# Order of the value products, a mask product with all its rows, and weights in smaller pieces, in a two-layer transformer block on one core

## The chip, the cores and the metric

The kernel runs on one core of a Trainium2 chip, as one program. TensorE multiplies matrices, VectorE, ScalarE and GpSimd do elementwise work, SyncE (SP) issues DMAs, and so does ScalarE's own queue. The metric is the device time of one execution in microseconds; the less the better.

## What is computed

Two layers over 512 latent tokens of width 1024 and 256 context tokens. Each layer normalises and modulates the tokens, projects them (`w_in`, 2976 columns) and splits the columns over four mixers of four heads of 64: latent attention (keys and values come from a narrow latent vector), retention forwards and backwards, neighbourhood attention on an 8 x 64 grid, and sliding-window attention with sink logits. Their outputs are joined and projected (`w_out`); a gated FFN of 2816 hidden units follows. The parts that the change touches:

```python
def softmax_attend(q, k, v, scale, sink=None):
    s = jnp.einsum('bhqd,bhkd->bhqk', q, k, preferred_element_type=jnp.float32) * scale
    ...
    p = jax.nn.softmax(s, axis=-1)
    ...
    return jnp.einsum('bhqk,bhkd->bhqd', p.astype(v.dtype), v)

def na_mixer(xq, xk, xv, yq, yk, yv, rpb):
    ...
    col_in = (c[None, :] >= c0[:, None]) & (c[None, :] < c0[:, None] + NA_KC)
    ...
    s_loc = jnp.where(col_in[:, None, :], s_loc, NEG_INF)
    ...

def reference(x, c, ctx, c_ctx, ada_w, ...):
    for l in range(DEPTH):
        ...
        mx, my = token_mixers(hx @ w_in[l], hy @ w_in[l], row, col, ...)
        x = x + gx1 * (mx @ w_out[l])
        hx = rms_norm(x, norm2_g[l]) * (1.0 + scx2) + shx2
        x = x + gx2 * swiglu(hx, ffn_w1[l], ffn_w3[l], ffn_w2[l])
        ...
    return rms_norm(x, final_norm_g)
```

## The kernel before, in words

Tokens come in six tiles of 128 (0 to 3 the grid, 4 and 5 the context); the last layer only finishes the four of the grid. All data is float32. Large products are made of three (`mm3`, L455 to L457): both operands are split into a rounded high part and a low remainder, and high times high, high times low and low times high are summed in PSUM. A weight comes into a `raw` buffer by DMA; `split_unit` then lets ScalarE make the high part `wh` (L435) and VectorE, each third time GpSimd, the low part `wl` (`sub_lo`, L201). `raw` has 2 buffers of 2048 elements a partition (1 MB), `wh` 5 and `wl` 7 of 1024.

The order in which a layer is written down: `na_proj` (the blocks of `w_in` for the neighbourhood's keys and values and for its queries), `na_attn`, `swa_proj`, `swa_attn`, `ret_proj`, `mla_proj` with the latent attention tile by tile, the output projection in parts between them (`rest`, `finish`), and the FFN in 11 groups of 256 hidden units (`tr_units` loads W1 and W3, then W2 follows). `load_nat` loads a block of `w_in` or `w_out` in two DMAs of up to four blocks of 128 rows each, from SP's queue; `tr_units` and the W2 load take ScalarE's. An engine executes its instructions in a fixed order, which a scheduler draws up when the program is built: it takes what is ready by its own reckoning, earlier written work first. So products of the next projection stand between the steps of an attention. A DMA that waits for a free buffer holds up what stands behind it on its queue.

Attention works on one tile of 128 queries and one head at a time: scores into PSUM, their minimum, the exponential on ScalarE (the scores carry a minus sign), the division by the sums (`norm_p`, L601), and `attend_T`, which transposes the probabilities block by block on TensorE (L567): ScalarE copies the first four blocks out of PSUM (L570), VectorE what comes after them (L572). When both heads of a pair have their transposed blocks `PTs`, `attend_pv` (L580) multiplies them with the values, the even head into the lower half of the output's partitions, the odd one into the upper half, so that each product has 64 stationary columns. There are 2, 4, 5 or 6 blocks of keys: 2 for context queries, 4 in the neighbourhood attention, 4 or 5 in the window, 6 in the latent attention.

In `na_attn` the columns outside the neighbourhood get a large number added to their score by a product (L918) of a 16-row indicator `naone` with a 16-row `namask`, behind the two products of queries and keys (L916, L917) and before those with the context's keys (L614). `swa_attn` does the like with the identity and `swmask`, of 128 rows (L1126, L1128), behind L1123 and L1124. Both masks are filled in `late_consts`.

Of the kernel before, what the change touches and what calls it, by code (L numbers as in the profile page):

```python
# [75 lines left out]

def build(tc, I, out, opts=None):
    nc = tc.nc
# [124 lines left out]
    # ---------------- constants  # L203
# [5 lines left out]
    naone = C("naone", [16, P], BF16)  # L209
    namask = C("namask", [16, 3, 32], BF16)  # L210
# [8 lines left out]
    def vec_tile(i, srcs):  # L219
        """rows of 128 values of the named vectors -> columns"""  # L220
        a = T("nat", [P, P])
        r = 0
        for name, src in srcs:
            n = src.shape[0] // P
            VROW[name] = (i, r)
            sp.dma_start(a[r:r + n, :], src.rearrange("(k p) -> k p", p=P))
            r += n
        ps = PS("u")
        pe.transpose(ps[:, 0:r], a[0:r, :], ident[0:r, 0:r])
        dve.tensor_copy(vecs[i], ps[:, 0:r])  # L230
# [5 lines left out]
    def late_consts():  # L236
        vec_tile(1, [("b1", I["ada_b"][1]), ("g1_1", I["norm1_g"][1]), ("g2_1", I["norm2_g"][1]),
                     ("qn0", I["mla_q_norm"][0]), ("kn0", I["mla_kv_norm"][0]),
                     ("qn1", I["mla_q_norm"][1]), ("kn1", I["mla_kv_norm"][1])])
        sp.dma_start(rope64, I["k_rope64"])  # L240
        sp.dma_start(rope32, I["k_rope32"])
        a = T("nat", [P, 96])
        sp.dma_start(a[0:16, :], I["k_namask"])
        act.activation(namask, a[0:16, :].rearrange("p (a b) -> p a b", a=3), AF.Copy)
        a = T("nat", [P, 2, P])
        sp.dma_start(a, I["k_swmask"])
        act.activation(swmask, a, AF.Copy)
        a = T("nat", [P, P])
        sp.dma_start(a[0:16, :], I["k_naone"])
        act.activation(naone, a[0:16, :], AF.Copy)  # L250
        act.activation(identb, ident, AF.Copy)
        s = I["swa_sink"]
        sp.dma_start(sink, bass.AP(tensor=s.tensor, offset=s.offset, ap=[[0, P], [H, LAYERS], [1, H]]))
        pool.tensor_scalar(sinkn, sink, -1.0, 1.0, op0=ALU.mult, op1=ALU.mult)

    # ---------------- small helpers
    def rsqrt(a, n, nm):
        """a [P, n] holds mean square; returns 1/sqrt(a)"""
        y = S("rs_y" + nm, n)
        u = S("rs_t" + nm, n)  # L260
        dve.tensor_scalar(y.bitcast(I32), a.bitcast(I32), 1, None, op0=ALU.logical_shift_right)
        dve.tensor_scalar(y.bitcast(I32), y.bitcast(I32), -1, 0x5F3759DF, op0=ALU.mult, op1=ALU.add)
        for _ in range(3):
            dve.tensor_tensor(u, y, y, op=ALU.mult)
            dve.scalar_tensor_tensor(u, u, -0.5, a, op0=ALU.mult, op1=ALU.mult)
            dve.scalar_tensor_tensor(y, u, 1.5, y, op0=ALU.add, op1=ALU.mult)
        return y

    def rsqrt1(a, nm):
        """a [P, 1]: 1/sqrt(a), times RS1"""  # L270
        y = S("rs_y" + nm, 1)
        u = S("rs_t" + nm, 1)
        dve.tensor_scalar(y.bitcast(I32), a.bitcast(I32), 1, None, op0=ALU.logical_shift_right)
        dve.tensor_scalar(y.bitcast(I32), y.bitcast(I32), -1, 0x5F3759DF, op0=ALU.mult, op1=ALU.add)
        for c in (-3.0, -12.0, -768.0):
            dve.scalar_tensor_tensor(u, y, a, y, op0=ALU.mult, op1=ALU.mult)
            dve.scalar_tensor_tensor(y, u, c, y, op0=ALU.add, op1=ALU.mult)
        return y

    # ---------------- adaLN modulation  # L280
# [5 lines left out]
    def mod_finish(l, v, s, k0, n):  # L286
        """bias, and for a scale (1 + scale) * g, of n feature blocks from k0"""
        m = modT[l][:, s, SLOT[v], k0:k0 + n]
        b = vec("b%d" % l, VT.index(v) * 8 + k0, n)
        dve.tensor_tensor(m, m, b, op=ALU.add)  # L290
        if v[1] == "c":
            dve.scalar_tensor_tensor(m, m, 1.0, vec("g%s_%d" % (v[2], l), k0, n), op0=ALU.add, op1=ALU.mult)
# [11 lines left out]
    def ada_first(q, ws):  # L304
        """shift and scale of the first norm of layer 0, features 256 * q and on"""
# [24 lines left out]
    def ada_rest(l, vs, wtag, depth, tag="u"):  # L330
        """vectors of layer l; a generator, a load and the products of an earlier load in each step"""
# [25 lines left out]
    def ada_sums(l, vs, wtag, depth, tag="u", atag="PT", after=None):  # L357
        """as ada_rest; the products are summed over the blocks of features before the tensor engine adds up partitions"""
# [72 lines left out]
    # ---------------- weights  # L431
# [7 lines left out]
    def load_nat(w, c0, n, ks=range(8)):  # L439
        """w [1024, *] DRAM -> list over k of (hi, lo) APs [128, n]"""  # L440
        res = []
        v = w.rearrange("(k p) n -> p k n", p=P)
        for kh in range(ks[0], ks[-1] + 1, 4):
            kn = min(4, ks[-1] + 1 - kh)
            raw = T("raw", [P, kn, n])
            Q["wn"].dma_start(raw, v[:, kh:kh + kn, c0:c0 + n])
            for u in range(0, kn, 2):
                hi, lo = split_unit(raw[:, u:u + 2, :], [2, n])
                for i in range(2):
                    res.append((hi[:, i, :], lo[:, i, :]))  # L450
        return res

    def mm3(ps, a, b, first, last):
        """ps += (a_hi + a_lo) (b_hi + b_lo)"""
# [4 lines left out]
    # ---------------- normalised, modulated, transposed activations  # L459
    def norm_stats(t, inplace=False):  # L460
        """normalised token tile t, as 8 blocks of 128 features"""
# [47 lines left out]
    def nat_block(w, c0, n, hT, order, rng=None, filler=None, nf=0, nxt=None):  # L509
        """generator over (t, psum) of natural outputs; rng(t) -> (a, b) columns wanted;  # L510
        nxt: first column and width of the block whose weights are loaded ahead"""
# [14 lines left out]
    def first_block(hT, order, parts):  # L526
        """as nat_block, all tiles together, the contraction in four parts"""
# [21 lines left out]
    def rope(out, ps, g, hd, t, tab):  # L549
        """out, ps: [P, g*hd] (out SBUF)"""  # L550
# [8 lines left out]
    # ---------------- softmax attention for one query tile and head  # L559
    def attend_T(Pm, nblk):  # L560
        """Pm [P, nblk*128] unnormalised -> its transposed blocks"""
# [13 lines left out]
    def attend_pv(pv, hp, PTs, vs):  # L575
        """heads 2 hp and 2 hp + 1 side by side: pv[:, 128 hp:128 hp + 128] = values^T of both"""
        n = len(vs[0])
        for i in range(n):
            for e in range(2):
                pe.matmul(pv[64 * e:64 * e + 64, hp * P:hp * P + P], vs[e][i], PTs[e][:, i, :],  # L580
                          start=(i == 0), stop=(i == n - 1), tile_position=(0, 64 * e))

    def norm_p(Pm, sums):
        """divide the rows by their sums, which come in parts [P, n]"""
# [18 lines left out]
    def put(pv, dst):  # L603
        """transposed outputs of 4 heads, two by two on the partitions, to dst [P, 2, 128]"""
# [5 lines left out]
    def scores(ps, q, k):  # L610
        """ps = q^T k from operands that are split and stacked: q, k lists of (stationary, moving)"""
# [4 lines left out]
    def soft_y(q_of, k_of, v_of, negsink=None, sk=None):  # L616
        """context queries of one tile: 4 heads on 256 keys"""
# [25 lines left out]
    def q_stack(src, scale):  # L643
        """src: 256 columns in DRAM -> stationaries [q_hi; q_hi], [q_lo; q_lo] of 4 heads, times scale"""
# [13 lines left out]
    def k_split(src, n, r=None):  # L658
        """src [P, n*64] natural, times r [P, 1] -> [P, n, 2, 64], hi and lo of each head"""
# [10 lines left out]
    def k_stack(dst, kd, n, t, tag="u"):  # L670
        """kd [P, n, 2, 64] natural, hi and lo -> dst[i][:, tile t] = [k_hi; k_lo]"""
# [6 lines left out]
    # ================= layers  # L678
# [31 lines left out]
    # startup  # L710
# [53 lines left out]
    # retention decays: log_sigmoid of both layers; [P, l, 8] and head-half layout [P, l, pair, dir]  # L764
# [27 lines left out]
    for l in range(LAYERS):  # L792
# [10 lines left out]
        # DRAM scratch of this layer  # L803
        o_d = DT(f"o_d{l}", [NT, 256])          # ret
        oT_d = DT(f"oT_d{l}", [512, NT])        # na | swa, transposed
        q_d = DT(f"q_d{l}", [NT, 640])          # mla: nope 256, rope 128 | swa 256
        qn_d = DT(f"qn_d{l}", [NT, 256])        # na, the grid in tiles of 16 columns
        r_d = DT(f"r_d{l}", [NT, 1280])         # ret q | k | v | gates f | gates b
        v_d = DT(f"v_d{l}", [NX, 256])          # na v of the grid
# [11 lines left out]
        def na_proj():  # L821
# [76 lines left out]
            def na_attn():  # L898
# [5 lines left out]
                for cb in range(4):  # L904
# [6 lines left out]
                    for h in range(H):  # L911
# [6 lines left out]
                        pe.matmul(loc, naone, namask[:, et:et + 1, :].to_broadcast([16, 8, 32]), start=False, stop=True)  # L918
# [23 lines left out]
        def mla_proj(R):  # L942
# [60 lines left out]
            def k_rope(t):  # L1003
                """the shared rope keys of the grid (t = 3) or of the context (t = 5)"""
# [277 lines left out]
        def m_pair(p, b):  # L1282
            """the operand of token tiles 2 p and 2 p + 1: b = 0 for mla | ret, 1 for na | swa"""
# [31 lines left out]
        # ---------- mixers  # L1315
# [22 lines left out]
        # ---------- output projection  # L1338
# [71 lines left out]
        # ---------- FFN  # L1410
# [17 lines left out]
        for g in range(11):  # L1428
            c0 = g * 256

            def tr_units(v):
                raw = T("raw", [P, 8, 256])
                Q["wf"].dma_start(raw, v[:, :, c0:c0 + 256])
                us = [split_unit(raw[:, 4 * u:4 * u + 4, :], [4, 256]) for u in range(2)]
# [31 lines left out]
            raw = T("raw", [P, 2, D])  # L1466
            Q["wf"].dma_start(raw, I["ffn_w2"][l, c0:c0 + 256, :].rearrange("(k p) n -> p k n", p=P))
            for j in range(2):
                down.append((gh[j], gl[j], split_unit(raw[:, j], [D])))
# [42 lines left out]
```

## Time and profile before

| what | value |
|---|---|
| median of 3 runs | 1955.18 us (1953.36 to 1959.28) |
| profiled execution, first to last instruction | 1949.8 us |
| median of the runs less that span | 5.4 us |
| TensorE busy | 1862.3 us, 96% |
| VectorE busy | 1205.8 us, 62% |
| ScalarE busy | 691.4 us, 35% |
| GpSimd busy | 614.8 us, 32% |
| moved by DMA | 215.46 MB, mean 111 GB/s |

The profiled execution's own time is known as its span from the first to the last instruction; what lies around it is taken as the distance to the runs' median. A busy time counts an engine's instructions and not its waits. The ends of matmuls are modelled and overlap, so their cost is better read from one start to the next. A float32 product of L580 stands in the trace as two matmuls. `po`, `pg`, `ps`, `pt`, `pu` are PSUM tiles, `PEld` is TensorE's load of the stationary operand, and `x22` says that 22 like instructions in a row were merged.

### The profile page before, as it was taken

To read this page: it belongs to the slowest core of one execution; us is meant where nothing else is said; L and a number is where in the kernel's file an instruction comes from. 1 tells how busy PE (TensorE), PEld (TensorE's weight loads), DVE (VectorE), ACT (ScalarE), POOL (GpSimd) and SP (SyncE) were. 2 spreads that over 40 slices of the span, in tenths; PEclk is the share of its full clock that TensorE was granted. 3 is DMA by queue.
4 is the path that set the end of the run, shared out by engine and by line. 5 is a ranking of instruction groups with operands and counts; after the bars stand their busy time and mean duration, and the time that the engine had idled before them with its cause. 6 is when DMAs were issued, how large, how long until landed. Compare 5 with 4: busy or idle time off the path is not lost.

```text
span 1949.8 us, 32084 instructions
## 1 busy us (share of the span) xinstructions
PE 1862.3 (96%) x12367; PEld 1604.1 (82%) x12367; DVE 1205.8 (62%) x2743; ACT 691.4 (35%) x1597; POOL 614.8 (32%) x571
## 2 busy tenths in 40 slices
PE   7999999899989999999999999999899999999997
PEld 3677776777789999999999977677687899999996
DVE  5787786776898767453434382464687864444345
ACT  3335643254542222212222243454254532222223
POOL 0211011423115544444344021111333043636442
PEclk9999999899999999999999999999999999999999
DMA  7765434453124345242211223223343032222321
GB/s 235 211 186 165 131 117 136 145 171 79 44 87 152 120 157 180 97 136 73 73 51 59 87 81 115 66 77 97 112 157 92 12 108 96 100 87 87 109 87 44
DMA packets 192034, 215.46 MB, mean 111 GB/s; under 512 B 65124, under 2 KB 140042, under 8 KB 191882
## 3 DMA queue, kind: packets, MB, share of 16 engines
q1 hardware_dynamic: 117098, 102.25, 17.2%
q10 hardware_dynamic: 74784, 111.16, 17.2%
q8 instruction: 97, 1.59, 0.3%
q14 instruction: 55, 0.45, 0.1%
HBM read 192.76 MB, written 20.63 MB: 109 GB/s over the span
## 4 chain that ended last, share of the span: by engine, by line
PE 66%; DVE 7%; issue 2%; ACT 2%; DMA 2%; POOL 1%; SPq 0%; DVEq 0%; ACTq 0%; POOLq 0%
PE ps L455 10%; PE ps L457 10%; PE ps L456 10%; PE pg L455 8%; PE pg L457 8%; PE pg L456 8%; PE po L580 3%; PE ps L614 2%; PE pt L567 2%; DVE wl L201 1%; DVE b L1227 1%; DVE nat L1341 1%; PE pt L650 1%; ACT wh L435 0%; DMA qn_d<-nat 0%
## 5 line engine op out<-in xcount | busy, mean ns | idle before, releaser
L456 PE MATMUL ps<-b,wh 128*128 128x256 f32 x1760 | 499.1, 284 | 2.2 <-DVE b L201 1.9
L455 PE MATMUL ps<-b,wh 128*128 128x256 f32 x1760 | 499.6, 284 | 0.0
L457 PE MATMUL ps<-b,wl 128*128 128x256 f32 x1760 | 498.9, 284 | 0.4 <-POOL wl L201 0.4
L455 PE MATMUL pg<-wh,b 128*128 128x512 f32 (+2 forms) x1128 | 442.5, 393 | 3.0 <-DVE b L1298 1.7
L457 PE MATMUL pg<-wh,b 128*128 128x512 f32 (+2 forms) x1128 | 440.2, 390 | 2.6 <-DVE b L201 1.4
L456 PE MATMUL pg<-wl,b 128*128 128x512 f32 (+2 forms) x1128 | 440.5, 390 | 0.8 <-POOL wl L201 0.6
L456 PEld LDWEIGHTS ps<-b,wh 128*128 128x128 f32 x1760 | 338.4, 192 | 3.4 <-DVE b L201 2.1
L455 PEld LDWEIGHTS ps<-b,wh 128*128 128x128 f32 x1760 | 338.1, 192 | 3.2 <-issue 2.0
L457 PEld LDWEIGHTS ps<-b,wl 128*128 128x128 f32 x1760 | 338.3, 192 | 0.6 <-POOL wl L201 0.6
L201 DVE TENSOR_TENSOR wl<-raw,wh 128x1024 fp32r<-128x1024 f32 (+1 forms) x130 | 197.9, 1526 | 200.8 <-ACT wh L435 191.9
L435 ACT ACTIVATE wh<-raw 128x1024 fp32r<-128x1024 f32 (+1 forms) x196 | 203.0, 1050 | 239.0 <-PE pg L457 169.5
L1343 POOL TENSOR_TENSOR b<-b,nat 128x512 f32<-128x512 f32 (+1 forms) x204 | 224.8, 1121 | 135.7 <-DVE nat L1341 92.4
L201 POOL TENSOR_TENSOR wl<-raw,wh 128x1024 fp32r<-128x1024 f32 (+1 forms) x66 | 164.8, 2496 | 289.6 <-ACT wh L435 278.9
L455 PEld LDWEIGHTS pg<-wh,b 128*128 128x128 f32 x1128 | 214.2, 190 | 43.7 <-issue 4.8
L457 PEld LDWEIGHTS pg<-wh,b 128*128 128x128 f32 x1128 | 214.1, 190 | 42.2 <-issue 4.2
L456 PEld LDWEIGHTS pg<-wl,b 128*128 128x128 f32 x1128 | 214.5, 190 | 37.0 <-issue 2.8
L1341 DVE TENSOR_TENSOR nat<-pg,gate 128x512 f32<-128x512 f32 x240 | 161.5, 686 | 85.2 <-PE pg L457 80.2
L1452 DVE TENSOR_TENSOR P<-ps,P 128x256 f32<-128x256 f32 x110 | 46.4, 423 | 140.6 <-PE ps L457 140.5
L1450 ACT ACTIVATE P<-ps 128x256 f32<-128x256 f32 x110 | 41.9, 382 | 242.3 <-PE ps L457 155.0
L1453 ACT ACTIVATE b<-P 128x256 fp32r<-128x256 f32 x110 | 45.7, 416 | 223.7 <-DVE P L1452 215.5
L201 POOL TENSOR_TENSOR b<-P,b 128x256 fp32r<-128x256 f32 x36 | 28.7, 798 | 282.0 <-ACT b L1453 282.0
L383 DVE SCALAR_TENSOR_TENSOR PT<-qT,consts,PT 128x512 f32<-128x512 f32 x112 | 96.8, 882 | 6.7 <-DMA qT<-in_ada_w_dram 5.5
(320 smaller groups left out, 2490.3 us busy)
## 6 DMA issues: line engine op xcount, KB each, us to landing
raw<-in_ffn_w_dram ACTq DMA_DIRECT2D x66, 1024.0 KB
qT<-in_ada_w_dram ACTq DMA_DIRECT2D x96, 256.0 KB
raw<-in_w_in_dram SPq DMA_DIRECT2D x18, 1024.0 KB
a<-in_ada_w_dram SPq DMA_DIRECT2D x32, 256.0 KB
a<-in_ada_w_dram ACTq DMA_DIRECT2D x32, 256.0 KB
xn<-in_ada_w_dram ACTq DMA_DIRECT2D x32, 256.0 KB
raw<-in_w_out_dram SPq DMA_DIRECT2D x8, 1024.0 KB
ldq<-q_d SPq DMA_DIRECT2D x40, 128.0 KB
```

Of the source, the lines that this page charges most:

```text
L201: eng.tensor_tensor(out, full, hi.bitcast(F32), op=ALU.subtract)
L383: dve.scalar_tensor_tensor(acc[s], w, sS[:, k, s:s + 1], acc[s], op0=ALU.mult, op1=ALU.add)
L435: act.activation(hi, raw_ap, AF.Copy)
L455: pe.matmul(ps, a[0], b[0], start=first, stop=False)
L456: pe.matmul(ps, a[0], b[1], start=False, stop=False)
L457: pe.matmul(ps, a[1], b[0], start=False, stop=last)
L580: pe.matmul(pv[64 * e:64 * e + 64, hp * P:hp * P + P], vs[e][i], PTs[e][:, i, :], start=(i == 0), stop=(i == n - 1), tile_position=(0, 64 ...
L1341: dve.tensor_tensor(tm, ps, gates[(0 if t < 4 else 2) + b], op=ALU.mult)
L1343: eng.tensor_tensor(ap, ap, tm[:, a:c], op=ALU.add)
L1450: act.activation(s1[j][:, sl], ps[:, 0:256], AF.Silu)
L1452: dve.tensor_tensor(s1[j][:, sl], ps[:, 0:256], s1[j][:, sl], op=ALU.mult)
L1453: act.activation(gh[j][:, sl], s1[j][:, sl], AF.Copy)
```

## The change

Three edits. The value products of a pair of heads run from the last block of keys to the first, and of each block the odd head first. `naone` and `namask` have 128 rows, of which all but the first 16 are zero. `raw` has 4 buffers of half the size, and every weight load moves at most 512 KB: two blocks of 128 rows of a `w_in` or `w_out` block, half of a W1 or W3 group, one of the two blocks of W2. Comments and docstrings are dropped too.

```diff
+CHANGED = {'pad': {'raw': 1024}, 'bufs': {'raw': 4}}
+
+def merged(opts):
+    r = dict(opts or {})
+    for k, v in CHANGED.items():
+        r[k] = {**r.get(k, {}), **v} if isinstance(v, dict) else v
+    return r
+
 def build(tc, I, out, opts=None):
+    opts = merged(opts)
...
-    naone = C("naone", [16, P], BF16)
-    namask = C("namask", [16, 3, 32], BF16)
+    naone = C("naone", [P, P], BF16)
+    namask = C("namask", [P, 3, 32], BF16)
...
-        act.activation(namask, a[0:16, :].rearrange("p (a b) -> p a b", a=3), AF.Copy)
+        pool.memset(namask, 0.0)
+        pool.memset(naone, 0.0)
+        act.activation(namask[0:16], a[0:16, :].rearrange("p (a b) -> p a b", a=3), AF.Copy)
...
-        act.activation(naone, a[0:16, :], AF.Copy)
+        act.activation(naone[0:16], a[0:16, :], AF.Copy)
...
     def load_nat(w, c0, n, ks=range(8)):
         res = []
         v = w.rearrange("(k p) n -> p k n", p=P)
-        for kh in range(ks[0], ks[-1] + 1, 4):
-            kn = min(4, ks[-1] + 1 - kh)
-            raw = T("raw", [P, kn, n])
-            Q["wn"].dma_start(raw, v[:, kh:kh + kn, c0:c0 + n])
-            for u in range(0, kn, 2):
-                hi, lo = split_unit(raw[:, u:u + 2, :], [2, n])
-                for i in range(2):
-                    res.append((hi[:, i, :], lo[:, i, :]))
+        for kh in range(ks[0], ks[-1] + 1, 2):
+            raw = T("raw", [P, 2, n])
+            Q["wn"].dma_start(raw, v[:, kh:kh + 2, c0:c0 + n])
+            hi, lo = split_unit(raw, [2, n])
+            for i in range(2):
+                res.append((hi[:, i, :], lo[:, i, :]))
         return res
...
     def attend_pv(pv, hp, PTs, vs):
         n = len(vs[0])
-        for i in range(n):
-            for e in range(2):
+        for i in reversed(range(n)):
+            for e in (1, 0):
                 pe.matmul(pv[64 * e:64 * e + 64, hp * P:hp * P + P], vs[e][i], PTs[e][:, i, :],
-                          start=(i == 0), stop=(i == n - 1), tile_position=(0, 64 * e))
+                          start=(i == n - 1), stop=(i == 0), tile_position=(0, 64 * e))
...
-                        pe.matmul(loc, naone, namask[:, et:et + 1, :].to_broadcast([16, 8, 32]), start=False, stop=True)
+                        pe.matmul(loc, naone, namask[:, et:et + 1, :].to_broadcast([P, 8, 32]), start=False, stop=True)
...
             def tr_units(v):
-                raw = T("raw", [P, 8, 256])
-                Q["wf"].dma_start(raw, v[:, :, c0:c0 + 256])
-                us = [split_unit(raw[:, 4 * u:4 * u + 4, :], [4, 256]) for u in range(2)]
+                us = []
+                for u in range(2):
+                    raw = T("raw", [P, 4, 256])
+                    Q["wf"].dma_start(raw, v[:, 4 * u:4 * u + 4, c0:c0 + 256])
+                    us.append(split_unit(raw, [4, 256]))
...
-            raw = T("raw", [P, 2, D])
-            Q["wf"].dma_start(raw, I["ffn_w2"][l, c0:c0 + 256, :].rearrange("(k p) n -> p k n", p=P))
             for j in range(2):
-                down.append((gh[j], gl[j], split_unit(raw[:, j], [D])))
+                raw = T("raw", [P, D])
+                Q["wf"].dma_start(raw, I["ffn_w2"][l, c0 + j * P:c0 + j * P + P, :])
+                down.append((gh[j], gl[j], split_unit(raw, [D])))
```

## Rows read from the trace of the kernel before

**Rows 1.** The page's part 1: busy us, share of the span, instructions.

```profile
PE 1862.3 (96%) x12367; PEld 1604.1 (82%) x12367; DVE 1205.8 (62%) x2743; ACT 691.4 (35%) x1597; POOL 614.8 (32%) x571
```

**Rows 2.** Busy us (instructions) by stage, TensorE first; last clock, DMA share, GB/s.

```profile
446.00:540.00 94.00, 93.37 (x643) 74.76 (x643) 69.77 (x186) 47.10 (x126) 18.55 (x20) 1.00 0.19 53
...
600.00:1140.00 540.00, 537.53 (x3837) 500.82 (x3837) 293.90 (x456) 118.86 (x208) 225.60 (x205) 1.00 0.32 106
```

**Rows 3.** TensorE's longest wait for a split weight: us, times, longest.

```profile
PE pg L456 <- POOL wl L201: 0.6, 1, 0.6
```

**Rows 4.** Timeline of TensorE: start us, us, line, tiles, shapes, count.

```profile
1307.40 0.39 PE L455 MATMUL pg<-wh,b 128*128 128x512 f32 x1
1307.63 0.40 PE L456 MATMUL pg<-wl,b 128*128 128x512 f32 x1
1307.96 0.43 PE L580 MATMUL po<-PT,b 128*64 128x128 f32 x2
1308.32 0.50 PE L457 MATMUL pg<-wh,b 128*128 128x512 f32 x1
```

**Rows 5.** Timeline of TensorE: first and last of 56 single value products.

```profile
148.44 0.43 PE L580 MATMUL po<-PT,b 128*64 128x128 f32 x2
...
1547.88 0.43 PE L580 MATMUL po<-PT,b 128*64 128x128 f32 x2
```

**Rows 6.** Timeline of TensorE: two stretches of value products.

```profile
1295.58 1.09 PE L580 MATMUL po<-PT,b 128*64 128x128 f32 x16
...
1299.44 1.09 PE L580 MATMUL po<-PT,b 128*64 128x128 f32 x14
```

**Rows 7.** Line L580: what ended idle time before it (us, times).

```profile
  ACT PT L570: 13.2, 41
```

**Rows 8.** Timeline: the copies of one head's transposed blocks.

```profile
497.01 0.60 ACT L570 ACTIVATE PT<-pt 128x512 f32<-128x512 f32 x1 [0.46 <-PE pt L567]
...
497.23 0.42 DVE L572 COPY PT<-pt 128x256 f32<-128x256 f32 x1 [0.69 <-PE pt L567]
```

**Rows 9.** Line L918: ns min/median/max, first and last start us, form.

```profile
L918 PE MATMUL ps<-consts x32: 277/278/389, 162.7 to 1273.3; 16*128 16x256 bf16 x32
```

**Rows 10.** Timeline of TensorE around one neighbourhood mask.

```profile
1245.08 0.28 PE L917 MATMUL ps<-b,qT 128*128 128x256 f32 x1
1245.29 0.28 PE L918 MATMUL ps<-consts 16*128 16x256 bf16 x1
1245.50 0.50 PE L614 MATMUL ps<-b,qT 128*128 128x256 f32 x2
1245.84 0.28 PE L917 MATMUL ps<-b,qT 128*128 128x256 f32 x1
```

**Rows 11.** Timeline of TensorE around one mask of the sliding window.

```profile
1290.26 0.28 PE L1124 MATMUL ps<-b,qT 128*128 128x256 f32 x1
1290.38 0.23 PE L1128 MATMUL ps<-consts 128*128 128x128 bf16 x1
1290.42 0.48 PE L614 MATMUL ps<-b,qT 128*128 128x256 f32 x2
1290.74 0.39 PE L457 MATMUL pg<-wh,b 128*128 128x512 f32 x1
```

**Rows 12.** DMA issues of the FFN weights: count and KB of each.

```profile
raw<-in_ffn_w_dram ACTq DMA_DIRECT2D x66, 1024.0 KB
```

**Rows 13.** Line L1433 on ScalarE's queue: ns min/median/max of an issue.

```profile
L1433 ACTq DMA_DIRECT2D raw<-in_ffn_w_dram x44: 374/375/1307, 447.8 to 1882.5; - x44
```

**Rows 14.** The chain that ended last: start us, us, what.

```profile
1142.72 5.18 DMA raw<-in_w_in_dram
...
1380.62 3.40 DMA raw<-in_mla_w_uq_dram
```

**Rows 15.** ScalarE's waits for weights: us, times, longest.

```profile
ACT wh L435 <- DMA raw<-in_ffn_w_dram: 19.8, 7, 3.4
...
ACT wh L435 <- DMA raw<-in_w_in_dram: 17.4, 8, 6.5
```

## The prediction

> **What bounds the kernel now.** I read the page's busy times first, then busy times by stage, then TensorE's waits, and last the matmul timeline where the changed lines run. Busy times show one engine near its limit: TensorE is busy 96% of the span, VectorE 62%, ScalarE 35% [rows 1]. By stage it is closer still: in the latent-attention stage of layer 0 (446 to 540 us) TensorE is busy 93.37 of 94 us beside VectorE's 69.77, in layer 0's FFN 537.53 of 540, both at a granted clock of 1.00 [rows 2]. So where the value products and the weight pieces run, an instruction taken from TensorE comes off the end, and one taken from another engine does not. TensorE hardly waits for weights: the largest wait for a split weight (wl) is 0.6 us in the whole span [rows 3]. In the timeline of matmuls the reader should look at the distance from one start to the next, since their ends are modelled.
>
> **The value products.** Two matmuls of the trace are one float32 product. In the old order the first product of a pair of heads needs only the even head's first transposed block, so it goes out early and by itself, and other work comes between it and the rest. A plain projection product follows the one before it by 0.23 us; with a single value product between two of them, the distances are 0.33 and 0.36, together 0.69 [rows 4]. The single product thus costs 0.69 - 0.23 = 0.46 us: its 0.36, and 0.10 of delay ahead of it. I count 56 such singles, the first at 148.44, the last at 1547.88 us [rows 5]; 60 pairs of heads are computed. In the new order the first product needs the odd head, which is the later one, so nothing of a pair of heads can go early, and the single joins the others. What does it cost there? A stretch of 16 (8 products) lasts 1.09 us, as one of 14 does [rows 6]: at best nothing. At worst it costs the mean of the stretch of 14, 1.09 / 7 = 0.16. A single then gives back 0.30 to 0.46 us, 56 of them 17 to 26 us.
>
> Against this stands a stall that the single filled. The weight loads of these products waited for ScalarE's copy of the transposed blocks at 41 places, 13.2 us in all [rows 7]. Were nothing else to fill the time there, only 56 - 41 = 15 singles would give back 0.46, 7 us. But projection products stand around the singles [rows 4] and the order of the engine is drawn up anew for the changed program, so other ready products can take that time. I take 19 us, in the upper half between 7 and 26, as TensorE is so full that moved filler is seldom missing.
>
> The new order also asks for the last block first. For five and six key blocks VectorE copies that block, ScalarE the first four. At one such place ScalarE's copy begins at 497.01 and takes 0.60, VectorE's begins at 497.23 and takes 0.42 [rows 8]: they end at 497.61 and 497.65, so asking for VectorE's first costs 0.04 us. Twenty-four pairs of heads have five or six blocks: 1 us, inside the 19. If the new order cuts off a first piece again there (VectorE's blocks early, then other work, then the rest), each keeps a switch of about the old 0.46: 24 x 0.46 = 11 us less gain, which the lower bound of 7 covers.
>
> **The mask.** 32 products have 16 rows [rows 9]. From one (L917) to the mask, from the mask to two score products and on to the next L917 the distances are 0.21, 0.21 and 0.34, together 0.76 us [rows 10]. The sliding window's mask has all 128 rows and 128 columns: the same sequence there takes 0.12, 0.04 and 0.32, together 0.48 [rows 11]. The new mask has 256 columns, twice as many; 128 more cost half of the 0.12 that a product of 256 takes [rows 11], 0.06. So 0.76 - 0.48 - 0.06 = 0.22 us each, 7 us. Below it is nothing, if the delay comes from the repeated reading of a 32-column mask instead of from its rows; above it is 0.28 x 32 = 9. I take 7, since the delay ahead of the mask (0.21 for 0.12) is that which the single value product has ahead of it, and those share a change of the array's shape and no repeated reading.
> The Trainium skill (TensorEngine Tiling (Array Packing), Performance Considerations) recommends row tiling for contractions of 64 rows or less, which speaks against filling 16 rows up to 128. By that rule this term would be zero at best and the sum 7 us higher, 1935; the trace differs, as the 16-row product is here the dearer one. Two fills of constants on GpSimd are new, once, at the start; GpSimd is busy 32% [rows 1], and the first mask product comes only at 162.7 us [rows 9].
>
> **The weights.** The same bytes, splits, order of splits and buffer space, but 96 more issues: FFN's 66 loads of 1 MB become 132 on ScalarE's queue [rows 12], and on SP's 22 of w_in and 8 of w_out become 60 (the first four of w_in have two blocks of 128 rows already and stay). An issue takes 0.375 us [rows 13], so ScalarE gets 66 x 0.375 = 25 us more. What hides them: ScalarE is busy 118.86 of 540 us in layer 0's FFN [rows 2]; without that cover they would cost up to 25. Behind an issue that waits for a slot stand ScalarE's weight casts and the activations of the up products, and TensorE waits for these; but a slot is now freed by one split, not two, so a first half is asked for earlier. At the start of layer 1 the chain holds 5.18 us of waiting for a 1 MB piece, and a 384 KB piece took 3.40 [rows 14]. The slope is (5.18 - 3.40) / 640 KB = 2.8 ns a KB, so 512 KB would take about 3.8: the first half is there 1.4 us earlier, and the end of two in series 2.4 later. The gain is bounded by 0.6 us of visible waits [rows 3] plus two such first halves, about 3; the loss at the start, where four free slots allow up to three pieces of w_in to go ahead of modulation weights, by 3 x 2.6 (half of 5.18) = 8. I take 1 us of gain: TensorE's waits bear out neither end.
>
> **The sum.** 19 + 7 + 1 = 27 us. The profiled span is 1949.8, so 1922.8 after; the median of the runs shown, 1955.2, lies 5.4 above that span, which I leave as it is: 1928.2, so 1928.
>
> **The rivals.**
> 1. *The singles only filled stalls.* The value part falls to 7 us or below and the mask to nothing or little: 1955 - 7 = 1948 with the mask at zero, 1941 with it. For it: the 41 waits of rows 7. Against: they are 0.3 us each, less than the single's 0.46, so even unfilled some is left.
> 2. *The pieces cost what the products save.* Each time that ScalarE stands waiting for a piece (7 times for FFN weights, 8 for w_in [rows 15]), the end of two halves in series comes 2.4 us later, and ScalarE's queue hands this to TensorE. All 15: 36 us, so 1955 - 26 + 36 = 1965, slower. It decides from 11 of the 15 on. For it: those waits exist. Against: FFN's TensorE is idle 2.5 us in 540 [rows 2], so most waits are hidden, and two halves are usually in flight together.
> The Trainium skill (DMA: Bandwidth & Descriptors, Bandwidth) advises batching transfers to at least 1 MiB, which is this rival's rule; no row here shows one weight load in two halves.
> 3. *No change.* A new order of all engines loses elsewhere, where TensorE waits for others, what it saves here: 1955. For it: the singles' removal shifts every later choice of the order. Against: TensorE is idle 4% of the span in all [rows 1], and what is lost would have to be new waits.
>
> **How the numbers follow.** Within 0.3% (about 5.9 us) a measurement of this kernel can't be told from no change: 1949.3 to 1961. My forecast, 1914 to 1941, has 0.64; rival 1 has 0.17, of which 0.15 under 1949 and 0.02 above; rival 3 has 0.08; rival 2 has 0.11, nearly all of it slower. Faster: 0.64 + 0.15 = 0.79, same 0.10, slower 0.11. The lowest end is 26 + 9 + 3 = 38 us: 1917, and a few lower for filler that fits better, 1913. Upward the range takes in rival 1 and part of 3: 1953. Outside are rival 2, half of 3 and a little below: 2 in 10.
>
> **What would show it.** Value products (L580's successor) in stretches of 8, 16, 20 and 24 without singles, the count of stretches of two falling from 56 to under 10; the distance from L917's successor to the next at most 0.55 us instead of 0.76; TensorE's busy time some 20 us lower, FFN's stages unchanged in length; 132 issues on ScalarE's queue with no new wait of TensorE for wl. I am wrong if singles reappear as pairs of VectorE's blocks, if the wait for the transposed blocks grows from 13 us to 30, or if FFN's 540 us grow by more than 5.

## The result and the profile after

The changed kernel takes 1927.45 us (median of 4 runs, 1925.95 to 1930.51) beside 1955.99 for the kernel before on the same chip: a ratio of 0.9853, 95% interval 0.9835 to 0.9871. The forecast was 1928. The sum came out, but not term by term: added one after the other, the weights come out 16 us worse than forecast and the value products 16 us better, and that the two cancel is luck.

The page's part 1 of the changed kernel, against [rows 1]:

```profile
span 1925.9 us, 32215 instructions
PE 1832.2 (95%) x12367; PEld 1596.9 (83%) x12367; DVE 1196.8 (62%) x2743; ACT 688.9 (36%) x1597; POOL 614.3 (32%) x573
```

TensorE is 30.1 us less busy, with as many instructions; the span is 23.9 us shorter. Here only 1.6 us lies between the span and the median; the span of before (1949.8) lies 6.2 us under the median of its four runs, so the spans show less of a gain than the medians do.

The timeline of TensorE in the changed kernel, against [rows 4] and [rows 6]: a stretch of ten products (x20) between two projection products, and one of eight (x16) between transposes.

```profile
1299.42 0.40 PE L468 MATMUL pg<-wl,b 128*128 128x512 f32 x1
1299.75 1.31 PE L592 MATMUL po<-PT,b 128*64 128x128 f32 x20
1300.99 0.76 PE L579 MATMUL pt<-consts,P 128*128 128x128 f32 x5
...
1256.36 1.09 PE L592 MATMUL po<-PT,b 128*64 128x128 f32 x16
1257.38 0.65 PE L579 MATMUL pt<-consts,P 128*128 128x128 f32 x4
```

No single product is left: 26 stretches of 16, 15 of 24, 13 of 8, 7 of 20, and one short one of 4 ahead of a stretch of 16 (at 254.82). One of the 8, at 507.56, is cut off in the same way ahead of one of 16, in a pair with six blocks. The 0.33 from the projection's start to the stretch's is still there, but once for a pair of heads instead of twice, and the full stretch of 16 runs 1.02 us from start to start: the product that joined it is free. Line L592's idle time, against [rows 7]:

```profile
  ACT PT L582: 9.7, 35
  DVE PT L584: 2.9, 10
```

The wait for the transposed blocks is 12.6 us where it was 13.2: taking the singles away has not made it longer.

Line L930, the mask, and the timeline around one, against [rows 9] and [rows 10]:

```profile
L930 PE MATMUL ps<-consts x32: 282/283/283, 164.4 to 1261.9; 128*128 128x256 bf16 x32
```

```profile
1249.82 0.28 PE L929 MATMUL ps<-b,qT 128*128 128x256 f32 x1
1249.94 0.28 PE L930 MATMUL ps<-consts 128*128 128x256 bf16 x1
1249.98 0.48 PE L626 MATMUL ps<-b,qT 128*128 128x256 f32 x2
1250.30 0.28 PE L929 MATMUL ps<-b,qT 128*128 128x256 f32 x1
```

The distances 0.12, 0.04 and 0.32 make 0.48 instead of 0.76 us, exactly those of the sliding window's mask [rows 11], although the mask's columns are twice as many.

So far all is gain. Layer 0's FFN is none: its window, against [rows 2], and two of TensorE's waits, against [rows 3] (us, times, longest):

```profile
600.00:1140.00 540.00, 533.54 (x3804) 498.18 (x3802) 288.98 (x448) 117.64 (x205) 221.42 (x204) 0.99 0.32 102
```

```profile
PE ps L467 <- ACT P L1464: 3.8, 1, 3.8
...
PE ps L469 <- POOL wl L213: 0.4, 1, 0.4
```

TensorE is idle 6.5 us in these 540 where it was 2.5, and the mean clock is 0.99. It does not wait for a weight; it waits for ScalarE's activation of the up products (L1464), and the timeline of the changed kernel shows what held that up:

```profile
719.37 2.52 POOL L213 TENSOR_TENSOR wl<-raw,wh 128x1024 fp32r<-128x1024 f32 x1
721.92 0.39 ACTq L1447 DMA_DIRECT2D raw<-in_ffn_w_dram  x1
722.36 0.38 ACT L1464 ACTIVATE P<-ps 128x256 f32<-128x256 f32 x1 [5.94 <-POOL wl L213]
722.79 0.58 PE L467 MATMUL ps<-b,wh 128*128 128x256 f32 x1 [3.83 <-ACT P L1464]
723.17 0.41 PE L468 MATMUL ps<-b,wh 128*128 128x256 f32 x1
723.39 0.41 PE L469 MATMUL ps<-b,wl 128*128 128x256 f32 x1
...
728.27 0.28 PE L469 MATMUL ps<-b,wl 128*128 128x256 f32 x1
728.39 0.28 PE L467 MATMUL ps<-b,wh 128*128 128x256 f32 x1
```

GpSimd's split ends at 721.89 and frees a slot of `raw`; only then can the DMA issue on ScalarE's queue run (721.92), and only behind it the activation (722.36) that empties the PSUM bank TensorE wants. After these 3.83 us without work the products follow each other by 0.21 us instead of 0.12: the granted clock in the windows from 722.79 to 728 is 0.50, the lower level of 1.2 GHz. That lasts 5.3 us, in which 22 products of 0.12 and two short ones start, some 2.9 us at full clock; so the wait costs 3.8 + 2.4 = 6.2 us. ScalarE does not wait longer for the pieces themselves. The issues of FFN weights, against [rows 12], and ScalarE's waits for pieces, against [rows 15]:

```profile
raw<-in_ffn_w_dram ACTq DMA_DIRECT2D x132, 512.0 KB
```

```profile
ACT wh L449 <- DMA raw<-in_w_in_dram: 9.0, 3, 6.7
...
ACT b L1467 <- DMA raw<-in_ffn_w_dram: 3.0, 1, 3.0
```

The weight casts wait 9.0 us for pieces, where they waited 37.2 for loads; none of the 9.0 is for an FFN weight. Layer 0's FFN takes 530.4 us from the first to the last activation of its up products, 522.6 before.

### The profile page after: what moved, and what is told of

Its sections match the earlier page's. It is cut to its first block, busy times and chain, and to the rows that moved or that the text cites. A ratio compares the mean times of both kernels' runs of the same rounds, so it can differ in the third digit from the quotient of the medians.

```text
span 1925.9 us, 32215 instructions
## 1 busy us (share of the span) xinstructions
PE 1832.2 (95%) x12367; PEld 1596.9 (83%) x12367; DVE 1196.8 (62%) x2743; ACT 688.9 (36%) x1597; POOL 614.3 (32%) x573
## 4 chain that ended last, share of the span: by engine, by line
PE 65%; DVE 8%; issue 2%; POOL 2%; DMA 1%; ACT 1%; SPq 0%; ACTq 0%; DVEq 0%; POOLq 0%
PE ps L467 10%; PE ps L468 10%; PE ps L469 10%; PE pg L469 8%; PE pg L467 8%; PE pg L468 8%; PE po L592 2%; PE ps L626 2%; PE pt L579 2%; DVE wl L213 1%; DVE nat L1353 1%; DVE PT L397 1%; DVE P L613 1%; DVE b L1239 1%; DMA qT<-in_ada_w_dram 0%
## 5 line engine op out<-in xcount | busy, mean ns | idle before, releaser
L1466 DVE TENSOR_TENSOR P<-ps,P 128x256 f32<-128x256 f32 x110 | 46.4, 422 | 129.6 <-PE ps L469 129.5
L1464 ACT ACTIVATE P<-ps 128x256 f32<-128x256 f32 x110 | 41.5, 383 | 213.4 <-PE ps L469 131.6
L397 DVE SCALAR_TENSOR_TENSOR PT<-qT,consts,PT 128x512 f32<-128x512 f32 x112 | 102.1, 927 | 19.3 <-DMA qT<-in_ada_w_dram 18.4
```

The costliest lines, as they stand in the source:

```text
L397: dve.scalar_tensor_tensor(acc[s], w, sS[:, k, s:s + 1], acc[s], op0=ALU.mult, op1=ALU.add)
L1464: act.activation(s1[j][:, sl], ps[:, 0:256], AF.Silu)
L1466: dve.tensor_tensor(s1[j][:, sl], ps[:, 0:256], s1[j][:, sl], op=ALU.mult)
```

## The experiments

Each time is the median of 4 to 12 runs; the ratio is to the kernel before on the same chip, whose medians were 1952 to 1956 us. Seven stretches of the span are cut at starts in the traces: A to layer 0's last value product, B to the first up activation, C to the last one of layer 0, D to layer 1's first mask, E to its first up activation, F to its last, G to the end. E holds layer 1's attention and A layer 0's. A cut does not fence work in: the scheduler can move products of a projection or an FFN across it, so a stretch can get shorter by giving work away.

| kernel | A | B | C | D | E | F | G | span |
|---|---|---|---|---|---|---|---|---|
| before | 538.7 | 27.5 | 522.6 | 141.6 | 332.1 | 341.0 | 46.3 | 1949.8 |
| pieces alone | 539.0 | 35.2 | 532.7 | 140.4 | 330.5 | 341.4 | 46.4 | 1965.6 |
| pieces and products | 533.2 | 29.0 | 531.0 | 139.0 | 318.1 | 336.2 | 46.4 | 1932.9 |
| changed (these and mask) | 527.9 | 29.0 | 530.4 | 140.2 | 315.7 | 336.2 | 46.5 | 1925.9 |
| pieces alone, SP | 534.6 | 35.1 | 517.8 | 141.3 | 332.8 | 341.6 | 46.4 | 1949.6 |
| pieces and products, SP | 531.1 | 30.2 | 522.1 | 138.8 | 319.1 | 340.5 | 45.2 | 1927.0 |
| changed, SP | 531.0 | 30.2 | 522.1 | 139.6 | 316.1 | 340.3 | 45.2 | 1924.5 |
| changed, layer 0 SP | 527.9 | 30.2 | 522.3 | 138.8 | 314.6 | 337.0 | 45.4 | 1916.2 |

Each row is one trace. Two kernels were traced twice: the other trace of the changed kernel has A 529.5, C 529.0, E 316.0 and F 336.2, that of the last row A 532.3, C 522.2, E 315.7 and F 337.0. The same kernel's A thus differs by up to 4.4 us from one trace to the next.

**Each part from the kernel before: pieces alone, mask alone, pieces with the product order.** The product order with 1 MB loads was not tried.

```diff
# pieces alone: load_nat, tr_units, W2 and raw as in the change, for example
-            raw = T("raw", [P, 2, D])
-            Q["wf"].dma_start(raw, I["ffn_w2"][l, c0:c0 + 256, :].rearrange("(k p) n -> p k n", p=P))
+                raw = T("raw", [P, D])
+                Q["wf"].dma_start(raw, I["ffn_w2"][l, c0 + j * P:c0 + j * P + P, :])
# mask alone
-                        pe.matmul(loc, naone, namask[:, et:et + 1, :].to_broadcast([16, 8, 32]), start=False, stop=True)
+                        pe.matmul(loc, naone, namask[:, et:et + 1, :].to_broadcast([P, 8, 32]), start=False, stop=True)
# pieces and products: the first, and
-        for i in range(n):
-            for e in range(2):
+        for i in reversed(range(n)):
+            for e in (1, 0):
```

> The weights in 512 KB pieces alone, products and mask as before. Theory: the pieces are no part of the gain. In the trace after, TensorE lost 3.83 us at 722 us to an activation that stood behind a piece's issue on ScalarE's queue, and layer 0's FFN got 7.8 us longer; the start of layer 1's FFN got 4.8 shorter. So between 1951 and 1964, best guess 1958. Rival, that the finer pieces bring part of the gain: 1950 or less, with the waits at the layers' starts shorter.

> The mask with 128 rows alone. Theory: each of 32 mask products gives back 0.76 - 0.48 = 0.28 us on a full TensorE, 9 us: 1947, range 1944 to 1951; the distances around it read 0.12, 0.04 and 0.32 as in the trace after. Rival, that the time is given back in stalls of the neighbourhood attention (VectorE's minimum and division are late next): the distances fall but the time stays above 1952.

> Weights in pieces and the new order of the value products, mask of 16 rows as before. Theory: less than the run with the weights alone by 17 to 26 us, best guess 21: 1937; no stretch of two matmuls of value products is left. Rival, that the singles filled stalls: less than the weights alone by 7 us or fewer.

Pieces alone: 1970.64 us, 1.0079 [1.0057, 1.0102], 15 us slower; a miss. Mask alone: 1948.43, 0.9962 [0.9943, 0.9981], 7 us as expected. Pieces and products: 1935.12, 0.9901 [0.9879, 0.9922]; the time was expected, its difference of 35.5 us to the pieces alone was not. TensorE's waits and the timeline with the pieces alone:

```profile
PE ps L453 <- ACT P L1450: 6.1, 2, 3.1
...
PE pu L390 <- ACT P L1450: 2.3, 1, 2.3
```

```profile
628.60 2.34 POOL L201 TENSOR_TENSOR wl<-raw,wh 128x1024 fp32r<-128x1024 f32 x1
630.97 0.37 ACTq L1433 DMA_DIRECT2D raw<-in_ffn_w_dram  x1
631.39 0.38 ACT L1450 ACTIVATE P<-ps 128x256 f32<-128x256 f32 x1 [4.98 <-POOL wl L201]
631.83 0.58 PE L453 MATMUL ps<-b,wh 128*128 128x256 f32 x1 [3.06 <-ACT P L1450]
```

It is the pattern of the changed kernel, three times, in layer 0's FFN (631.83, 740.83, 848.00), twice with the clock down behind it. C grows by 10.1 us and B by 7.7. B's growth is work and not waiting. The lines of B before and with the pieces alone show TensorE with 190 products instead of 150, idle 2.2 us instead of 1.8:

```profile
538.70:566.20 27.50, 25.73 (x150) 22.25 (x147) 26.43 (x63) 12.49 (x24) 5.17 (x3) 1.00 0.23 78
```

```profile
539.00:574.20 35.20, 33.04 (x190) 28.13 (x187) 34.85 (x85) 15.36 (x32) 7.50 (x4) 1.00 0.23 76
```

They came from A and C, so C's loss on equal work is larger than 10.1 us.

**The pieces issued from SP's queue.** If it is the issue that holds up ScalarE's activations, it must go away when SP issues the same pieces.

```diff
-'q': {'wf': 'act',
+'q': {'wf': 'sp',
```

> The weights in pieces alone, with the FFN's issues on SP's queue instead of ScalarE's. Theory: what made the pieces alone 15 us slower sits on ScalarE's queue, where an issue that waits for a slot holds the up product's activation, and TensorE then waits 3 us at a time (3.06, 3.08 and 2.32 us at three places of layer 0's FFN). On SP nothing of that kind stands behind an issue: 10 us less than the pieces alone, 1960, range 1953 to 1964, and no wait of TensorE for the activation. Rival, that the loss is in the pieces' number or transfer itself, or that SP's queue is blocked instead: 1967 or more.

1953.85 us, 0.9989 [0.9975, 1.0003]: in the sum the whole loss is gone, 17 us by the queue alone. The window of layer 0's FFN with the pieces alone, from ScalarE's queue and then from SP's:

```profile
574.00:1107.00 533.00, 519.83 (x3773) 488.97 (x3774) 296.27 (x424) 114.14 (x196) 222.70 (x206) 0.99 0.33 105
```

```profile
569.00:1088.00 519.00, 515.75 (x3781) 485.28 (x3781) 299.57 (x425) 115.76 (x198) 220.92 (x207) 1.00 0.33 108
```

TensorE's idle time falls from 13.2 to 3.3 us and the clock is whole; C loses 14.9 us. B stays at 35, with the same 190 products. C is now also 4.8 us shorter than before, with 23 products fewer. Loads of 1 MB from SP's queue were not run, so what the queue is worth without the pieces stays open.

**Which half of the new order counts: odd head first (blocks first to last), or last block first (even head first).** Both from the changed kernel.

```diff
# heads only
-        for i in reversed(range(n)):
+        for i in range(n):
# start and stop turned round with it
# blocks only
-            for e in (1, 0):
+            for e in (0, 1):
```

> The changed kernel with the key blocks running from first to last again, and only the odd head ahead of the even one. Theory: what matters is that the first product needs the later head; the order of the blocks is worth nothing: 1927, range 1923 to 1932, no singles. Rival, that the last block first is what keeps a pair of heads together: singles or split stretches at the 24 pairs with five or six blocks, and 1933 or more.

> The changed kernel with the even head first again, the key blocks still from last to first. Theory: the first product then needs only the even head, so the singles are back, over 50 stretches of two, and the time is 25 to 35 us above the changed kernel, best guess 1955. Rival, that the block order carries the gain: no more than 5 us above it.

Heads only: 1931.34 us, 0.9874 [0.9845, 0.9903], no singles; not to be told from the changed kernel. Blocks only: 1953.72, 0.998 [0.9965, 0.9995], and 53 singles are back, as this one between projection products in its timeline:

```profile
1306.15 0.40 PE L456 MATMUL pg<-wl,b 128*128 128x512 f32 x1
1306.48 0.43 PE L580 MATMUL po<-PT,b 128*64 128x128 f32 x2
1306.84 0.50 PE L457 MATMUL pg<-wh,b 128*128 128x512 f32 x1
```

The gain is in asking for the later head first; the order of the blocks is worth nothing that shows.

**Masks of 64 rows**, zero from row 16, in the changed kernel: is it the number of zero rows, or the array being whole?

```diff
-    naone = C("naone", [P, P], BF16)
-    namask = C("namask", [P, 3, 32], BF16)
+    naone = C("naone", [64, P], BF16)
+    namask = C("namask", [64, 3, 32], BF16)
```

> The changed kernel with masks of 64 rows instead of 128. Theory: any product that does not use all rows changes the shape of the array and pays before and after it: distances of 0.21, 0.21 and 0.34 again and 9 us more than the changed kernel, 1936, range 1932 to 1940. Rival, that 16 rows were too few in themselves: 0.12, 0.04, 0.32 and 1927.

1935.07 us, 0.9894 [0.9878, 0.991]: 8 us lost. Its timeline has the distances of 16 rows, 0.21, 0.21 and 0.34:

```profile
1249.80 0.28 PE L929 MATMUL ps<-b,qT 128*128 128x256 f32 x1
1250.01 0.28 PE L930 MATMUL ps<-consts 64*128 64x256 bf16 x1
1250.22 0.50 PE L626 MATMUL ps<-b,qT 128*128 128x256 f32 x2
1250.56 0.28 PE L929 MATMUL ps<-b,qT 128*128 128x256 f32 x1
```

**The changed kernel, and pieces with products, from SP's queue** (the edit as above).

> The changed kernel with the FFN's issues on SP's queue. Theory: the 3.83 us wait at 722 us goes and layer 0's FFN shrinks from 530 to about 523: 1920, range 1916 to 1924. Rival, that SP's other loads (modulation vectors, gates, the loads of the next layer) are held behind pieces that wait for a slot: 1928 or more, with new waits at the starts of the layers.

> The kernel before with two edits, the 512 KB pieces and the new order of the value products; the FFN weights are issued from SP's queue instead of ScalarE's, and the mask is the old one of 16 rows. Beside the pieces alone from SP's queue (1953.9 us) it shows what the product order is worth where the pieces cost nothing. Theory A, the order takes away the singles and nothing else, 53 x 0.46 us = 24: 1930 us, and no single products in the trace. Theory B, the order is worth 35 us wherever it stands, as it was on top of the pieces from ScalarE's queue: 1919 us. The changed kernel from SP's queue took 1926.9 us with the mask's 7 us in it, which points to 1934; so I expect 1929 to 1936.

Changed: 1926.93 us, 0.9851 [0.9836, 0.9866], the same as the changed kernel; a miss. C gives the 8 us back (522.1), but the time does not. A is 3.1 us longer, no more than two traces of one kernel differ by. E and F together are 4.5 us longer; that F alone takes 4.1 is in part work that stayed in it, 2439 products instead of 2408. Why C's gain does not reach the end, no run settles. Pieces with products: 1930.55, 0.9891 [0.9874, 0.9908]. Beside the pieces alone from SP, on another chip, the product order is worth 0.0098 of 1954, 19 us with some 4 either way by the intervals, not 35: the time is theory A's, the size a little under its 24.

**Layer 0's FFN weights from SP's queue, layer 1's from ScalarE's**, since C is shorter with the one and F with the other; then once more beside the changed kernel.

```diff
-                    Q["wf"].dma_start(raw, v[:, 4 * u:4 * u + 4, c0:c0 + 256])
+                    (sp if l == 0 else act).dma_start(raw, v[:, 4 * u:4 * u + 4, c0:c0 + 256])
# and so for W2
```

> The changed kernel, with the FFN weights of layer 0 issued from SP's queue and those of layer 1 from ScalarE's as before. Theory A: each layer keeps the length that it had with its queue, layer 0's FFN 522 us (first to last activation of the up products, 530 in the changed kernel) and layer 1's 336 (340 from SP's queue): 4 us less than all from SP's queue, 1923 us. Theory B: the order of the whole program is drawn up anew with each move, and what one stage gains another loses: 1927 us, the same as both. A: 1920 to 1924, B: 1925 to 1930; I give A a little more.

> The changed kernel itself, beside the next run on the same chip. In its own call it stood at a ratio of 0.9853, the kernel with layer 0's FFN weights on SP's queue at 0.9848, but the kernel before stood 3 us apart in those two calls (1956.0 and 1952.3 us). I expect 0.985; if the mixed queues are worth their 8 us in layer 0's FFN, this run is 3 to 5 us above the next one, otherwise the same within 2 us.

> The changed kernel with layer 0's FFN weights issued from SP's queue and layer 1's from ScalarE's, beside the changed kernel on the same chip. Theory A (each layer keeps the FFN length that it has with its queue, 8 us less in layer 0, and 2 to 4 us are lost ahead of it): 3 to 5 us under the changed kernel. Theory B (what the FFN gains is lost elsewhere): the same within 2 us. The spans of the two traces, 1921.4 and 1925.9 us, speak for A.

1923.28 us, 0.9848 [0.9833, 0.9864] the first time. The second time 1921.15, 0.9822 [0.9795, 0.9848], beside 1927.71, 0.986 [0.9835, 0.9885], for the changed kernel: 6.6 us less, where 3 to 5 were expected, and no run of the one (1917.95 to 1923.98) reaches the other's (1925.63 to 1936.26). The traces agree: C is 522.2 and 522.3, F 337.0 in both, each about as with its better queue. But the intervals of the two ratios overlap, and the first time the ratio was only 0.0005, 1 us, under that of the changed kernel. So it is the best version of these by 1 to 7 us, and no more is shown.

## Why the prediction was right in its sum

**What bounds the kernel** held, with a reservation. A and E together are 27.2 us shorter after the change, against 19 + 7 = 26 forecast for the products and masks that stand there, but they do not hold the same work. These are A, E and F before and then after, TensorE's busy us and products (x) first:

```profile
0.00:538.70 538.70, 501.90 (x3068) 378.54 (x3068) 400.68 (x1120) 241.62 (x650) 107.09 (x120) 0.99 0.48 147
1230.40:1562.50 332.10, 310.66 (x2068) 253.79 (x2068) 227.19 (x673) 159.66 (x419) 69.57 (x69) 0.98 0.28 87
1562.50:1903.50 341.00, 340.75 (x2443) 323.49 (x2442) 155.14 (x215) 97.07 (x152) 167.52 (x143) 1.00 0.28 94
```

```profile
0.00:527.90 527.90, 484.85 (x3063) 373.31 (x3064) 396.54 (x1117) 239.30 (x650) 106.62 (x122) 0.98 0.51 152
1227.50:1543.20 315.70, 298.59 (x2107) 252.66 (x2106) 228.76 (x694) 161.15 (x425) 68.72 (x72) 0.98 0.30 91
1543.20:1879.40 336.20, 335.12 (x2408) 317.98 (x2409) 146.04 (x199) 95.55 (x148) 170.05 (x144) 1.00 0.31 96
```

E has 39 products more and F 35 fewer, so F's 4.8 us are work that moved and no gain. Taken together, TensorE is busy 17.1 us less in A and 17.7 less in E and F: 34.8 us (31.9 with the other trace of the changed kernel), about what 56 singles at 0.46 and 32 masks at 0.28 come to, 34.7. Not all of it reaches the end: TensorE's idle time grows from 36.8 to 43.1 us in A and falls from 21.4 to 17.1 in E.

**The value products, 19 us.** Right in the mechanism; the size depends on what stands beside it. By the runs it is 19 us where the pieces do no harm, 25 where the changed kernel gets the even head first again, and 35 on top of the pieces from ScalarE's queue. TensorE's busy time falls by 31 us with either queue (1871.4 to 1840.2 and 1866.2 to 1835.3 us), more than the 24 that 53 singles at 0.46 make; what the other 7 are stays open. The spans fall by 32.7 and 22.6, since from SP's queue 8.3 us of it come back as idle time of TensorE in A (35.5 to 43.8 us). Stretches A and E alone lose 18.2 us (from ScalarE's queue) and 17.2 (from SP's), 0.34 and 0.32 for each of 53 singles, inside the 0.30 to 0.46 of the working; but 36 and 12 more products stand in them after it, so these are low. What B (6.2) and F (5.2) lose of the 32.7 goes with 30 and 23 products fewer in them. Of the first pieces that might have come back, from VectorE's blocks, there are two, of 4 and 8 matmuls.

**The masks, 7 us.** The right mechanism, a little small: 0.28 each instead of 0.22, 9 us by the timeline, 7 and 8 by the two runs (mask alone, 64 rows). The 0.06 for 128 more columns was charged and is not paid. That the delay goes with the rows and not with the repeated reading is shown by the 64-row mask, which has the reading of the full one and the distances of the 16-row one. The Trainium skill (TensorEngine Tiling (Array Packing), Key Properties) says that a change of tiling mode drains TensorE. If a product of 16 or 64 rows counts as such a change, the trace agrees: each mask that leaves the full array costs 0.28 us, and 64 rows pay as much as 16.

**The weights, 1 us of gain: the step that failed.** Both its bounds, 3 us of gain by visible waits and 8 of loss at the start of a layer, look for a late weight. The loss, 15 us for this part alone, goes away with ScalarE's queue, which the prediction had named ("Behind an issue that waits for a slot stand ScalarE's weight casts and the activations of the up products") and then dismissed with "a slot is now freed by one split, not two, so a first half is asked for earlier". The rows that showed the danger stood in the kernel before, among ScalarE's waits, where only those for DMA were read:

```profile
ACT P L1450 <- DVE wl L201: 38.5, 7, 6.9
...
ACT P L1450 <- POOL wl L201: 27.0, 4, 9.9
```

Eleven times, 65.5 us, the activation stood behind an issue that waited for a split. TensorE had slack for nearly all of it: its weight loads waited 0.4 us for this activation in all. With the pieces alone it is sixteen times and 69.7 us, hardly more, so the total is no price; what changes is where the waits fall. In layer 0's FFN they were these, before and then with the pieces alone:

```profile
  DVE wl L201: 15.3, 3
```

```profile
  POOL wl L201: 24.9, 5
  DVE wl L201: 21.6, 4
```

Three of 15.3 us in sum have become nine of 46.5, and at three of the nine TensorE has no slack left. In layer 1 eight became seven, and F keeps its length (341.0 and 341.4). From SP's queue these waits are gone from ScalarE. In the changed kernel only one long wait of TensorE is left of the three, with 6.2 of C's 7.8 us; most of the rest goes with two stretches of some 3 us at a granted clock of 0.50 (from 567.8 and 936.5), behind waits of 2.2 us each. My own mark, "if FFN's 540 us grow by more than 5", was passed: 7.8 in layer 0.

**The sum.** Added one after the other by their runs, pieces, products and masks are worth -15, +35 and +9 us, where the forecast had +1, +19 and +7 (other sequences, as products with 1 MB loads, were not run). The errors of the first two are 16 us each and cancel: that the sum came out is luck. With the pieces issued from SP's queue the same three are +2, +19 and +8, close to the forecast term by term, and the time is the same as the changed kernel's. The queue thus costs 17 us with the old product order, 2 with the new one and nothing that shows with the masks too, although C is 8 to 9 us longer from ScalarE's queue in these two. The order of the engines is drawn up anew for each program; what makes up for C there, no run settles. In spans the gain is 23.9 us, by the medians 28.5 (25 to 32 by the interval); the medians are the better measure, as each span is one execution.

**The rivals.** Rival 1 (singles only filled stalls) falls: 53 singles back cost 25 us (0.998 against 0.9853), and the wait for the transposed blocks is 16.3 us with them (ScalarE's and VectorE's copies, 9.6 and 6.7) and 12.6 without. Rival 2 (the pieces cost what the products save) had the right victim and the wrong cause: the pieces alone are slower, but no two transfers in series lie behind it: the changed kernel's weight casts wait less for pieces than before, and the same pieces from SP's queue cost nothing in the sum. The Trainium skill's rule of at least 1 MiB a transfer (DMA: Bandwidth & Descriptors, Bandwidth) does not decide here for the same reason: 512 KB pieces from SP stand at 0.9989 [0.9975, 1.0003]. Rival 3, a new order that loses elsewhere what it saves, was seen in the small, in the changed kernel from SP's queue, whose C is 8.3 us shorter and whose time is the same.

## What to carry to other kernels

Where one engine both issues DMAs and empties PSUM, read its waits for whatever frees the DMA's buffer, not only its waits for DMA: an issue that waits for a slot is a wait of everything behind it. Ask first for the operand that is ready last, so that a group of products with another array shape stays in one piece. Check a forecast stage by stage, since terms with wrong signs can make a right sum, and count the instructions of each stage, since a stage can also get shorter by giving work away.

## What was not expected of the hardware

A product of 16 or of 64 rows costs 0.28 us more than one of all 128 rows that stands in its place, and the full one of 256 columns adds no more to the sequence than one of 128 (0.48 us both). A wait of TensorE can cost more than its length: after 3.83 us idle the granted clock was 0.50 for 5.3 us, 2.4 us more, and after 3.06 us idle in the run with the pieces alone the products follow each other by 0.21 us for 3.4. It is not the length of the one wait alone that decides: after a wait of 2.2 us that ended at 566.6 the changed kernel's clock was 0.50 from 567.8 to 571, while after one of 3.3 us that ended at 577.7 the kernel before kept 1.00, and so did the pieces alone after 2.32 us (848.00).
